# Pooling and three of four Q/K projections as seven products of quartered matrices, made ahead of attention

## The chip, the cores and the metric

One core of a Trainium2 chip runs the whole kernel. The metric is device time in microseconds (us) for one execution. The core's engines are TensorE (PE, matmul; its weight loads are listed as PEld), VectorE (DVE), ScalarE (ACT), GpSimd (POOL) and SyncE (SP, which issues most of the DMAs). Each takes its own instructions in the order of the program and waits at semaphores for the others.

## The reference, cut

```python
# x: 1 x 1024 x 1024, 8 heads of 64, 4 pooling groups of 128, D_FF = 2816, float32
h = rmsnorm(x, norm1_g)
proj = h @ w_in                       # [q | k | v | f_logit | u]
log_f = log_sigmoid(f_logit + b_forget); c = cumsum(log_f)
logits = q.k / 8 + c_t - c_s          # causal; p = softmax(logits)
attn = p @ v                          # per head
pooled_g = window_sum(u_g, w) / count - u_g     # w = 2, 4, 8, 16, one per group
pool = (pooled_g @ w_pool[g]) * pool_scale
x = x + concat(attn, pool) @ w_out
x = x + (silu(h2 @ w_gate) * (h2 @ w_up)) @ w_down        # h2 = rmsnorm(x, norm2_g)
y = rmsnorm(x, final_g)
```

## The kernel before

Every float32 operand of a matmul is split into a high part (an ACT copy into a rounded type) and a low part (source minus high, by DVE or POOL: `split`). A product is then three matmuls, `mm3`: high by high, high by low and low by high. A matmul has 128 rows of weights and moves up to 512 columns.

The stages, in order of time:

1. Rows of x are normalised, transposed and split into `hTh` and `hTl` (128 x 8 x 1024: eight chunks of the model's width, all 1024 frames). Beside this PE makes v for heads 0 to 3 and the forget logits `fl` (line L374).
2. Four pooling groups, `group_project`: for each, two halves of 512 frames by 8 chunks by 3 matmuls (48). Their sliding sums (`group_pool`) and splits run on DVE and POOL, the small matmuls by `w_pool` are `mix`, and `decay` makes the running sums of the forget gates, which go to DRAM as `augd`.
3. `project(0)` makes Q and K of the first pair of heads: two kinds, two halves, 8 chunks, 3 matmuls (96). The result is scaled and split; DMAs from SBUF to SBUF bring it into the stacks `s1` and `s2`, which hold high and low parts and `augd` rows one above the other, so that a score is two matmuls.
4. Attention: `attend(p, fill, counts)` runs eight jobs for each pair. A job is scores, minimum, exponential, normalisation, transposes and values. Between its steps it takes matmuls out of a generator, the fill, as many as `counts` says for each job. The fills are `project(1)`; `project(2)` and the rest of v; `project(3)`; and the first output rows, o4 and o6.
5. The remaining output rows, second norm and transposes.
6. Gate and up projections by seven products of quartered matrices, and the down projection, to the end.

The instructions of an engine run in the order in which the program has them. It follows the order of the code, moved by a scheduler where `issue_after` or a dependency asks for it. SP's queue is one of these orders: a DMA that waits for a buffer holds up all that stand behind it. `wmask` is a 128 x 1024 tile with the causal edge that every softmax reads (at L620).

Of the kernel before, what the change touches and what calls it, by code (L numbers as in the profile page):

```python
# [8 lines left out]
F32 = mybir.dt.float32  # L9
# [6 lines left out]
P = 128  # L16
# [29 lines left out]
def tile_kernel(  # L46
# [41 lines left out]
    def bank(name, tag, bufs, n=1):  # L88
# [26 lines left out]
    augd = dram.tile([H, 2 * AUG, S], F32, name="augd")  # L115

# [94 lines left out]

    with pool("early", "right") as ep:
        xts = {}

        def e2(name, dt=F32):
            return ep.tile([P, HALO + S], dt, tag="e2", bufs=9, name=name)

        def xload(tt):
            xts[tt] = ep.tile([P, D], F32, tag="x", bufs=4, name=f"x{tt}") if tt < 4 else e2(f"x{tt}")[:, 0:D]
            nc.sync.dma_start(out=xts[tt], in_=xf[tt * P : (tt + 1) * P, :])  # L220
# [7 lines left out]
        g8, gcol = e2("g8")[0:ND, 0:P], e2("gcol")[:, 0:ND]  # L228
# [16 lines left out]
        for tt in range(2, NT):  # L245
            xload(tt)
            if tt == 3:
                nc.sync.dma_start(out=bfb, in_=b_forget[0].partition_broadcast(P))
        junk = ep.tile([P, D], mybir.dt.bfloat16, name="junk")
# [22 lines left out]
        fl = ep.tile([P, NT, H], F32, name="fl")  # L272
# [108 lines left out]
        with tc.issue_after(mark["rstd"].ins):  # L381
            nc.gpsimd.dma_start(out=pscale, in_=pool_scale[0].rearrange("(g p) -> p g", p=P))


        def ft(name):
            return ep.tile([P, NT, H], F32, name=name)
# [20 lines left out]
        def decay():  # L407
            lfT = []
            for a in range(2):
                lfT.append(bank(f"lf{a}", "t", 4))  # L410
                for tt in range(4):
                    nc.tensor.transpose(lfT[a][0:H, tt * P : (tt + 1) * P], fs[:, 4 * a + tt, :], ident)
            def row(name, dt=F32):
                return ep.tile([P, S], dt, tag="x", bufs=4, name=name)[0:H, :]

            one, cc = row("one"), row("cc")
            zero = wmask[0:H, 0:512]
            chl = [row("chi", R), row("clo", R)]
            with tc.issue_after(mark["rstd"].ins):
                nc.gpsimd.memset(one, 1.0)  # L420
            for a in range(2):
                nc.vector.tensor_tensor_scan(
                    cc[:, a * 512 : (a + 1) * 512], lfT[a][0:H, :], zero,
                    0.0 if a == 0 else cc[:, 511:512], ALU.add, ALU.add,
                )
            split(chl[0], chl[1], cc)
            for n in range(2):
                chl.append(row(("nhi", "nlo")[n], R))
                nc.scalar.activation(out=chl[2 + n], in_=f32(chl[n]), func=AF.Copy, scale=-1.0)
            rows = [one, one, f32(chl[2]), f32(chl[3]), f32(chl[0]), f32(chl[1]), one, one]  # L430
            for n, row in enumerate(rows):
                (nc.sync if row is one else nc.gpsimd).dma_start(out=augd[:, n, :], in_=row)


        def mix(g):
            (ph, pl), (wph, wpl) = phl[g], wps[g]
            for tb in range(2):
                ts = slice(tb * 512, (tb + 1) * 512)
                ps = bank(f"m{g}_{tb}", *(("s", 4) if g > 1 else rotate("tp", 2)))
                mm3(ps, wph, wpl, ph[:, ts], pl[:, ts], True, True)  # L440
                if g > 1:
                    mo = e2(f"mo{g}_{tb}")[:, 0:512]
                else:
                    mo = ap_.tile([P, 512], F32, tag="th", bufs=4, name=f"mo{g}_{tb}")
                nc.scalar.activation(out=mo, in_=ps, func=AF.Copy, scale=pscale[:, g : g + 1])
                nc.sync.dma_start(out=mixd[NPAIR + g, :, ts], in_=mo)

        us, pfs, phl, wps = {}, {}, {}, {}

        def group_project(g, mid=None):  # L450
            with tc.issue_after(copies[NT - 1 if g < 3 else NT - 3].ins):
                wh, wl = wsplit(wpool, w_in_r[:, :, U0 + g * P : U0 + (g + 1) * P], f"u{g}", eng=nc.gpsimd)
            wh, wl = chunk(wh, P), chunk(wl, P)
            wpr = ep.tile([P, P], F32, tag="wpr", bufs=2, name=f"wpr{g}")
            nc.sync.dma_start(out=wpr, in_=w_pool[0, g])
            wpp, nb = (ep, 2) if g > 1 else (hpool, 2)
            wps[g] = [wpp.tile([P, P], R, tag=t, bufs=nb, name=f"{t}{g}") for t in ("wph", "wpl")]
            with tc.issue_after(copies[NT - 1].ins):
                split(*wps[g], wpr, nc.gpsimd)
            u = us[g] = e2(f"u{g}")  # L460
            nc.vector.memset(u[:, 0:HALO], 0.0)
            for tb in range(2):
                ts = slice(tb * 512, (tb + 1) * 512)
                ps = bank(f"u{g}_{tb}", "s", 4)
                for c in range(ND):
                    mm3(ps, wh[:, c, :], wl[:, c, :], hTh[:, c, ts], hTl[:, c, ts], c == 0, c == ND - 1)
                nc.scalar.activation(out=u[:, HALO + tb * 512 : HALO + (tb + 1) * 512], in_=ps, func=AF.Copy)
                if mid and tb == 0:
                    mid()

        def group_pool(g, eng):
            u, w = us[g], WINDOWS[g]
            prev, d = u, 1
            while d < w:
                nxt = e2(f"us{g}_{d}")
                if 2 * d < w:
                    nc.vector.memset(nxt[:, 0:HALO], 0.0)
                eng.tensor_tensor(
                    out=nxt[:, HALO:], in0=prev[:, HALO:], in1=prev[:, HALO - d : HALO + S - d], op=ALU.add
                )  # L480
                prev, d = nxt, 2 * d
            pf = pfs[g] = e2(f"pf{g}") if g > 1 else pf01[:, g, :]
            nc.vector.scalar_tensor_tensor(
                out=pf[:, HALO:S], in0=prev[:, 2 * HALO :], scalar=1.0 / w, in1=u[:, 2 * HALO :],
                op0=ALU.mult, op1=ALU.subtract,
            )
            nc.vector.tensor_tensor(
                out=pf[:, 0 : w - 1], in0=prev[:, HALO : HALO + w - 1], in1=rcount[:, 0 : w - 1], op=ALU.mult
            )
            nc.vector.tensor_scalar(  # L490
                out=pf[:, w - 1 : HALO], in0=prev[:, HALO + w - 1 : 2 * HALO], scalar1=1.0 / w, scalar2=None,
                op0=ALU.mult,
            )
# [936 lines left out]
```

## Time and profile before

| what | value |
|---|---|
| median of 3 runs | 1035.37 us (1034.99 to 1035.57) |
| span of the profiled execution | 1033.6 us |
| PE busy | 1024.3 us, 99% |
| DVE, ACT, POOL busy | 632.8, 454.2, 381.1 us |
| v done, groups begin | 38.8 us |
| attention with its fills, about | 118 to 350 us |
| gate and up | 410 to 818 us |

The span runs from the first to the last instruction of one profiled execution; the time of a run is taken around the whole execution. The profiled execution's own time is not listed apart from its span. A matmul's busy time in the rows overlaps with that of the next one, so what one costs is read from the distance between starts. In the rows, "out<-in" are the program's tiles, the number behind an engine's stretch is its busy time, and square brackets tell how long the engine had been idle and what ended it.

### The profile page before, as it was taken

To read this page: it belongs to the slowest core of one execution; us is meant where nothing else is said; L and a number is where in the kernel's file an instruction comes from. 1 tells how busy PE (TensorE), PEld (TensorE's weight loads), DVE (VectorE), ACT (ScalarE), POOL (GpSimd) and SP (SyncE) were. 2 spreads that over 40 slices of the span, in tenths; PEclk is the share of its full clock that TensorE was granted. 3 is DMA by queue.
4 is the path that set the end of the run, shared out by engine and by line. 5 is a ranking of instruction groups with operands and counts; after the bars stand their busy time and mean duration, and the time that the engine had idled before them with its cause. 6 is when DMAs were issued, how large, how long until landed. Compare 5 with 4: busy or idle time off the path is not lost.

```text
span 1033.6 us, 14202 instructions
## 1 busy us (share of the span) xinstructions
PE 1024.3 (99%) x5104; PEld 868.9 (84%) x5104; DVE 632.8 (61%) x1000; ACT 454.2 (44%) x733; POOL 381.1 (37%) x312
## 2 busy tenths in 40 slices
PE   9999999999999999999999999999999999999997
PEld 7988888998888888888888888888888888888886
DVE  7565566776886479744433334334334789788886
ACT  7434355665665257533333233233233343333346
POOL 4350121213346043447537536636637510000045
PEclk9999999999999999999999999999999999999999
DMA  7224434333643134343143143143236755353424
GB/s 251 53 47 143 105 81 103 84 102 89 224 175 106 49 136 129 103 143 112 62 132 113 62 133 112 64 131 113 81 113 251 248 204 175 110 198 97 153 92 163
DMA packets 108439, 130.21 MB, mean 126 GB/s; under 512 B 7369, under 2 KB 70353, under 8 KB 108369
## 3 DMA queue, kind: packets, MB, share of 16 engines
q1 hardware_dynamic: 96544, 108.18, 33.4%
q10 hardware_dynamic: 11504, 20.47, 5.2%
q8 instruction: 40, 0.66, 0.2%
q0 software_dynamic: 320, 0.66, 0.2%
q14 instruction: 31, 0.25, 0.1%
HBM read 86.29 MB, written 33.03 MB: 115 GB/s over the span
## 4 chain that ended last, share of the span: by engine, by line
PE 98%; DMA 1%; ACT 0%; DVE 0%; POOL 0%; issue 0%; ACTq 0%; POOLq 0%
PE gu_P L161 14%; PE gu_P L162 14%; PE gu_P L163 14%; PE d L161 7%; PE d L162 7%; PE d L163 7%; PE po L657 4%; PE tp L643 3%; PE o L161 3%; PE o L162 3%; PE qk L161 3%; PE qk L162 3%; PE qk L163 3%; PE o L163 3%; PE v L374 2%; PE z L618 2%
## 5 line engine op out<-in xcount | busy, mean ns | idle before, releaser
L121 DVE TENSOR_TENSOR gu_P_l<-s,gu_P_h 128x1024 fp32r<-128x1024 f32 (+1 forms) x48 | 66.5, 1393 | 98.6 <-ACT gu_P_h L120 98.5
L162 PE MATMUL d<-d,d 128*128 128x512 f32 (+1 forms) x308 | 119.5, 388 | 0.0
L163 PE MATMUL d<-d,d 128*128 128x512 f32 (+1 forms) x308 | 119.5, 388 | 0.0
L629 POOL TENSOR_SCALAR p<-p,rr 128x128 f32<-128x128 f32 (+3 forms) x64 | 48.6, 764 | 175.5 <-DVE rr L628 140.2
L161 PE MATMUL d<-d,d 128*128 128x512 f32 x308 | 107.8, 388 | 0.0
L120 ACT ACTIVATE d<-r_f 128x1536 fp32r<-128x1536 f32 (+1 forms) x28 | 38.8, 1384 | 117.6 <-PE d L162 101.6
L121 DVE TENSOR_TENSOR gu_P_l<-r,gu_P_h 128x1024 fp32r<-128x1024 f32 x32 | 48.9, 1527 | 64.3 <-ACT gu_P_h L120 64.3
L1063 POOL TENSOR_TENSOR s<-r 128x1024 f32<-128x1024 f32 x10 | 24.0, 2401 | 161.9 <-DMA r<-in_w_up_dram 116.0
L120 ACT ACTIVATE gu_P_h<-r 128x1024 fp32r<-128x1024 f32 x32 | 33.8, 1060 | 91.1 <-PE gu_P L162 35.5
L162 PEld LDWEIGHTS d<-d,d 128*128 128x128 f32 x308 | 57.8, 188 | 12.0 <-DVE d L121 0.2
L161 PEld LDWEIGHTS d<-d,d 128*128 128x128 f32 x308 | 57.8, 188 | 12.0
L163 PEld LDWEIGHTS d<-d,d 128*128 128x128 f32 x308 | 57.8, 188 | 11.9
L626 ACT ACTIVATE p<-p,mn 128x128 f32<-128x128 f32 (+3 forms) x64 | 49.3, 772 | 32.8 <-DVE mn L620 29.9
L1291 POOL TENSOR_SCALAR sse<-sse 128x1 f32<-128x1 f32 x7 | 3.5, 494 | 158.1 <-ACT junk L1287 158.1
L1150 POOL TENSOR_TENSOR h<-h,qh 128x512 f32<-128x512 f32 x33 | 44.3, 1345 | 32.3 <-ACT qh L1148 24.1
L648 DVE TENSOR_TENSOR tl<-tp,th 128x512 fp32r<-128x512 f32 (+1 forms) x80 | 49.3, 632 | 10.7 <-ACT th L647 9.7
L120 ACT ACTIVATE gu_P_h<-s 128x1024 fp32r<-128x1024 f32 (+1 forms) x48 | 47.0, 984 | 19.7 <-PE gu_P L162 13.0
L1147 DVE TENSOR_TENSOR qh<-gu_P,sn_sU 128x512 f32<-128x512 f32 x22 | 15.2, 690 | 60.5 <-POOL h L1150 43.2
L121 DVE TENSOR_TENSOR d<-r_f,d 128x1536 fp32r<-128x1536 f32 (+1 forms) x28 | 45.7, 1633 | 10.5 <-ACT d L120 10.5
L163 PE MATMUL qk<-hTh,l_qk 128*128 128x512 f32 x128 | 50.7, 396 | 0.0
L161 PE MATMUL qk<-hTh,h_qk 128*128 128x512 f32 x128 | 50.6, 395 | 0.0
L162 PE MATMUL qk<-hTl,h_qk 128*128 128x512 f32 x128 | 50.4, 394 | 0.0
(337 smaller groups left out, 3067.1 us busy)
## 6 DMA issues: line engine op xcount, KB each, us to landing
r_f<-hsdP SPq DMA_DIRECT2D x77, 256.0 KB
r_wd<-in_w_down_dram SPq DMA_DIRECT2D x22, 512.0 KB
hsdP<-f ACTq DMA_DIRECT2D x43, 256.0 KB
r<-in_w_gate_dram SPq DMA_DIRECT2D x21, 512.0 KB
r<-in_w_up_dram SPq DMA_DIRECT2D x21, 512.0 KB
s<-hi SPq DMA_DIRECT2D x64, 128.0 KB
hsdP<-h ACTq DMA_DIRECT2D x32, 256.0 KB
x<-in_x_dram SPq DMA_DIRECT2D x8, 512.0 KB
```

The source lines that it names most:

```text
L120: mark["hi"] = nc.scalar.activation(out=hi, in_=src, func=AF.Copy)
L121: return eng.tensor_tensor(out=lo, in0=src, in1=f32(hi), op=ALU.subtract)
L161: nc.tensor.matmul(ps, lh, rh, start=start, stop=False, **kw)
L162: nc.tensor.matmul(ps, lh, rl, start=False, stop=False, **kw)
L163: mark["mm"] = nc.tensor.matmul(ps, ll, rh, start=False, stop=stop, **kw)
L626: nc.scalar.activation(out=pr[:, :n], in_=pr[:, :n], func=AF.Exp, scale=-1.0, bias=mn, accum_out=rs)
L629: nc.gpsimd.tensor_scalar(out=pr[:, :n], in0=pr[:, :n], scalar1=rr, scalar2=1.0, op0=ALU.mult, op1=ALU.mult)
L643: nc.tensor.transpose(tp[:, w : w + P], probs[h, 2 * sb + a][:, s * P : (s + 1) * P], ident)
L648: nc.vector.tensor_tensor(out=tl[:, :w], in0=tp[:, :w], in1=f32(th[:, :w]), op=ALU.subtract)
L657: mark["pv"] = nc.tensor.matmul(po[:, first * P : 2 * P], vt[p][:, s, j, :], part[:, o : o + wd], start=(s == 0 and part is th), stop=(s = ...
L1063: g(out=s1, in0=a21, in1=a22, op=ALU.add)
L1150: nc.gpsimd.tensor_tensor(out=h, in0=h, in1=q, op=ALU.mult)
```

## The change

The four pooling groups, two at a time, and the Q and K columns of a pair of heads are taken as one 256-column weight block each. Its 2 x 2 quarters (two column halves, two halves of the model's width) and those of the transposed h (two halves of the width, two halves of the frames) are multiplied by seven products instead of eight. A product is 4 chunks by 3 matmuls. There are five such units: a (groups 3 and 2), b (groups 1 and 0), c (pair 0), e (pair 2) and f (pair 3). Together 420 matmuls replace 480. Pair 1 keeps `project(1)`.

- The right-hand sums and differences t1 to t4 of h's quarters are made once (`block_steps`): t1, t2 and t4 on DVE, t3 on POOL, their high parts on ACT, their low parts on DVE and (half of t3) POOL.
- The weight sums of a unit (`unit_sums`) are four 128 x 512 operations on POOL, for c on DVE. Each product's page is split by ACT and POOL (`unit_page`), three of them with the low part on DVE (`LOWS`).
- PSUM results are put together in SBUF by ACT copies and DVE additions (`unit_step`). For c, e and f `done` scales and splits each quarter and stores it to DRAM (`qkd`). The high part goes through `stage`, two halves of `wmask`; the mixed pooling outputs go through the same halves.
- `load_stacks` loads the stacks from `qkd`, eight DMAs for a head and a half of the frames; for pair 0 these are 32, issued ahead of attention.
- The causal edge of `wmask` is written at the stage's end instead of the kernel's start.
- The fills of attention move up: `project(1)`, then the rest of v, then o4 and o6 in steps of one `mm3`; their pages are prepared in halves of 512 on POOL.

```diff
+    GROUPS_OF = dict(a=(3, 2), b=(1, 0))
+    PAIR_OF = dict(c=0, e=2, f=3)
...
+    def unit_sums(u, eng):
...
+        eng.tensor_tensor(out=s1, in0=a21, in1=a22, op=ALU.add)
+        eng.tensor_tensor(out=a21, in0=a11, in1=a21, op=ALU.subtract)
+        eng.tensor_tensor(out=a11, in0=s1, in1=a11, op=ALU.subtract)
+        eng.tensor_tensor(out=a12, in0=a12, in1=a11, op=ALU.subtract)
...
+        n = page_count[0] % 3
+        page_count[0] += 1
+        if n == 2:
+            t = mid.tile([P, 2, 512], R, tag="page", bufs=1, name=f"w{u}_{k}")
+        else:
+            t = wpool.tile([P, 2, 512], R, tag="wl", bufs=2, name=f"w{u}_{k}")
+        pages1[u, k] = t
+        split(t[:, 0, :], t[:, 1, :], src, LOWS.get((u, k), nc.gpsimd))
...
+    MOVING = dict(P1=(0, 0), P2=(1, 0), P3=(1, 1), P6="t2", P5="t1", P7="t3", P4="t4")
...
+        for c in range(4):
+            ws = slice(c * P, (c + 1) * P)
+            mm3(ps, t[:, 0, ws], t[:, 1, ws], bh[:, c, :], bl[:, c, :], start and c == 0, stop and c == 3, True)
...
+    def stage(dt):
...
+        t = wmask[:, 512 * n : 512 * n + 512] if not late_stage or n == 0 else late_stage[0]
...
+        nc.scalar.activation(out=hi, in_=c, func=AF.Copy, scale=sc)
+        nc.vector.scalar_tensor_tensor(
+            out=low, in0=c, scalar=sc, in1=f32(hi), op0=ALU.mult, op1=ALU.subtract
+        )
+        for to, of_ in zip(qkd[f, PAIR_OF[u]], (hi, low)):
+            nc.sync.dma_start(out=to[:, ts], in_=f32(of_))
...
+        def difference(eng, tmp, b, a, q):
+            (bh, bl), (ah, al) = of(*b, q), of(*a, q)
+            return [go(eng, tmp, bh, ah), go(eng, tmp, tmp, bl, ALU.add), go(eng, tmp, tmp, al)]
...
+            mo = stage(F32)
+            nc.scalar.activation(out=mo, in_=ps, func=AF.Copy, scale=pscale[:, g : g + 1])
+            nc.sync.dma_start(out=mixd[NPAIR + g, :, ts], in_=mo)
...
+    FREE, BOUND = ("P1", "P2", "P3"), ("P6", "P5", "P7", "P4")
+    work = [("a", k) for k in FREE] + [("c", k) for k in FREE] + [(u, k) for k in BOUND for u in "ac"]
+    work += [(u, k) for u in "eb" for k in FREE + BOUND] + [("f", k) for k in BOUND + ("P1", "P3", "P2")]
...
-    attend(0, project(1), [5, 4, 4, 3, 8, 6, 6, 0])
-    attend(1, both(project(2), project_v23()), [10, 7, 6, 8, 10, 8, 12, 0])
...
-    attend(2, project(3, first_chunk), [5, 2, 1, 6, 14, 7, 7, 1])
...
-    attend(3, fill, [3, 3, 4, 4, 4, 4, 3, 2], drain=False)
...
+    attend(0, project(1), [5, 4, 4, 3, 6, 5, 5, 0])
...
+    attend(1, project_v23(), [5, 4, 5, 5, 4, 5, 4, 0], events=[
...
+    attend(2, fill, [3, 3, 4, 4, 5, 5, 5, 3], drain=False, events=[
...
+    attend(3, fill, [0, 3, 4, 5, 5, 5, 6, 5], drain=False, events=[
```

The places that matter below, as the program orders them. First DVE, from the last forget logit on. Before (the f... rows are the polynomial of the gates):

```order
L379 TENSOR_TENSOR fl<-v_7_567,bfb 128x8
L389 TENSOR_SCALAR fa<-fl 128x64
L403 TENSOR_SCALAR fm<-fl 128x64
L390 TENSOR_TENSOR fa<-fa,fl 128x64
L392 TENSOR_SCALAR fz_601<-fe 128x64
```

After, at the same place (sum_t4h and sum_t are sums of h's quarters, t1l and t2l low parts of such sums, wa_P a page of unit a):

```order
L411 TENSOR_TENSOR fl<-v_7_574,bfb 128x8
L557 TENSOR_TENSOR sum_t4h<-hTh 128x1024 x2
L604 TENSOR_SCALAR fa<-fl 128x64
L618 TENSOR_SCALAR fm<-fl 128x64
L557 TENSOR_TENSOR sum_t4h<-sum_t4h,hTl 128x1024 x2
```

and, some rows on:

```order
L557 TENSOR_TENSOR sum_t_618<-hTh,sum_t4h 128x1024
L608 RECIPROCAL fz_967<-fz_967 128x64
L572 TENSOR_TENSOR t1l_610<-sum_t4h,t1h_609 128x1024
L427 TENSOR_TENSOR r_c_148<-r_c_148 128x512
L557 TENSOR_TENSOR sum_t_617<-sum_t_617,hTl 128x1024
L126 TENSOR_TENSOR wa_P_730<-r_a_144,wa_P_730 128x512
```

The small rows of the gates now stand between 15 operations of 1024 columns, which end with t2l.

On POOL, from the first group's page on. Before (l_u is a page's low part, us the sliding sums):

```order
L121 TENSOR_TENSOR l_u_781<-r_u_778,h_u_780 128x1024
L478 TENSOR_TENSOR us_1_762<-u_642 128x1024
L478 TENSOR_TENSOR us_2_765<-us_1_762 128x1024
L478 TENSOR_TENSOR us_4_768<-us_2_765 128x1024
L478 TENSOR_TENSOR us_8_771<-us_4_768 128x1024
L121 TENSOR_TENSOR l_u_895<-r_u_892,h_u_894 128x1024
```

After (wc_P are pages of unit c, sum_t4l is t3's sum, t3l its low part):

```order
L126 TENSOR_TENSOR wc_P_659<-r_c_148,wc_P_659 128x512
L557 TENSOR_TENSOR sum_t4l<-sum_t4l,hTl 128x1024
L126 TENSOR_TENSOR wc_P_681<-r_c_148,wc_P_681 128x512
L557 TENSOR_TENSOR sum_t4l<-sum_t4l,hTl 128x1024 x3
L126 TENSOR_TENSOR wc_P_710<-r_c_148,wc_P_710 128x512
L572 TENSOR_TENSOR t3l_614<-sum_t4l,t3h_613 128x1024
L126 TENSOR_TENSOR wc_P_792<-r_c,wc_P_792 128x512
```

Four pages of 1024 have become a run of pages of 512 with t3's sums among them, and the sliding sums have left POOL.

On SP, at the way into attention. Before (s are the stacks, hi the scaled high part of Q or K in SBUF):

```order
L569 DMA s_0_1_0_1248<-hi_1_0_1363 64x512
L570 DMA s_0_1_0_1250<-hi_1_0_1363 64x512
L569 DMA s_0_1_1_1249<-hi_1_0_1363 64x512
L570 DMA s_0_1_1_1251<-hi_1_0_1363 64x512
L569 DMA s_0_1_0_1248<-hi_1_1_1557 64x512
```

After, the page load and the first of the 32 stack loads (qk_0h and qk_0l are pair 0's results in DRAM):

```order
L243 DMA r_f_1176<-in_w_in_dram 128x4x128
L173 DMA r_qk_1_1634<-in_w_in_dram 128x8x128
L782 DMA s_0_0_0_1470<-qk_0h 64x512
L783 DMA s_0_0_0_1470<-qk_0l 64x512
L784 DMA s_0_0_0_1471<-qk_0h 64x512
L785 DMA s_0_0_0_1471<-augd 4x512
```

and what stands behind the 32nd (qk_3h and qk_3l are f's results):

```order
L498 DMA qk_3h<-wmask 128x512
L498 DMA qk_3l<-r_f 128x512
L829 DMA s_0_1_0_1642<-augd 4x1024
L829 DMA s_0_1_1_1643<-augd 4x1024
L498 DMA qk_3h<-wmask 128x512
L498 DMA qk_3l<-r_f 128x512
L668 DMA mixd<-wmask 128x512 x2
```

The stores that empty `wmask` stand behind all loads of the stacks. The r_qk load reads into the buffer whose last reader is the page of f's P2.

PE at that place, after (fP is f's last product, z scores, qk_1 the fill):

```order
L168 MATMUL fP_1513<-hTh,wf_P_1510 128x512
L897 MATMUL z_0_0_1598<-s_1_0_0_1476,s_0_0_0_1470 128x128
L898 MATMUL z_0_0_1598<-s_1_0_0_1477,s_0_0_0_1471 128x128
L897 MATMUL z_1_0_1609<-s_1_0_0_1476,s_0_0_0_1470 128x256
L898 MATMUL z_1_0_1609<-s_1_0_0_1477,s_0_0_0_1471 128x256
L166 MATMUL qk_1_0_1646<-hTh,h_qk_1_1630 128x512
```

Four score matmuls are all that stands between the last product and the fill's first matmul.

584 lines of the change are left out of this document (398 added, 186 removed).

## The prediction

> **What bounds the kernel now.** I read the page's summary first, then the stretches of the span, then single instructions around the place of the change, and last the rows that price what the change adds.
>
> ```profile
> span 1033.6 us, 14202 instructions
> PE 1024.3 (99%) x5104; PEld 868.9 (84%) x5104; DVE 632.8 (61%) x1000; ACT 454.2 (44%) x733; POOL 381.1 (37%) x312
> PE 98%; DMA 1%; ACT 0%; DVE 0%; POOL 0%; issue 0%; ACTq 0%; POOLq 0%
> ```
>
> PE is 99% busy and the chain that ends last runs on it for 98%, so a matmul taken away is worth its time as long as nothing else starts to make PE wait. The stretches (each engine's busy us) show how much room the others have:
>
> ```profile
> core 0: us, PE busy (x) PEld busy (x) DVE busy (x) ACT busy (x) POOL busy (x), PEclk, DMA share, GB/s
> 0.00:41.00 41.00, 38.53 (x285) 35.30 (x286) 25.88 (x61) 27.11 (x62) 21.77 (x51) 1.00 0.61 191
> 41.00:66.00 25.00, 25.00 (x112) 20.66 (x111) 9.93 (x32) 4.73 (x8) 13.79 (x6) 1.00 0.08 22
> 66.00:90.00 24.00, 24.00 (x112) 19.78 (x110) 18.79 (x29) 12.14 (x16) 2.09 (x4) 1.00 0.33 87
> 90.00:128.00 38.00, 38.00 (x181) 32.01 (x180) 19.16 (x42) 15.04 (x28) 2.92 (x5) 1.00 0.49 130
> 128.00:348.00 220.00, 220.00 (x1380) 198.29 (x1379) 154.68 (x411) 128.16 (x273) 69.40 (x69) 1.00 0.39 114
> 410.00:818.00 408.00, 408.00 (x1802) 337.84 (x1801) 173.66 (x174) 145.57 (x194) 218.58 (x116) 1.00 0.36 120
> ```
>
> From 41 to 348 us PE never waits, and DVE and POOL are lightly used ahead of attention. The stage that already uses seven products, 410 to 818, fills PE too, with 174 + 219 = 392 us of DVE and POOL in 408.
>
> **What is saved.** Starts of matmuls price one of 512 columns:
>
> ```profile
> 38.84 0.40 PE L161 MATMUL u<-hTh,h_u 128*128 128x512 f32 x1
> ...
> 41.42 0.16 DVE L379 TENSOR_TENSOR fl<-v,bfb 128x8 f32<-128x8 f32 x1
> 41.61 0.39 PE L161 MATMUL u<-hTh,h_u 128*128 128x512 f32 x1
> ```
>
> Twelve steps lie between 38.84 and 41.61, so one costs 0.231 us. The four groups (4 x 48) and pairs 0, 2 and 3 (3 x 96) were 480 matmuls; five units of seven products of 12 are 420. 60 x 0.23 = 13.8 us saved. Everything from the last output rows on is unchanged and costs nothing.
>
> **What the product stage adds.** Ahead of attention now stand 420 + 24 = 444 matmuls and 8 small transposes: 444 x 0.23 + 0.6 = 102.7, from 38.84 to 141.5 us if nothing waits. DVE and POOL feed it. Their prices:
>
> ```profile
> 61.67 1.21 DVE L483 SCALAR_TENSOR_TENSOR pf<-us,u 128x1008 f32<-128x1008 f32 x1 [13.81 <-POOL us L478]
> 62.80 2.37 DVE L487 TENSOR_TENSOR pf<-us,rcount 128x15 f32<-128x15 f32 x1
> ...
> 65.20 1.20 DVE L478 TENSOR_TENSOR us<-u 128x1024 f32<-128x1024 f32 x1
> ...
> 66.35 0.15 DVE L494 TENSOR_TENSOR pf<-pf,u 128x16 f32<-128x16 f32 x1
> ```
> ```profile
> 61.81 3.32 POOL L121 TENSOR_TENSOR l_u<-r_u,h_u 128x1024 fp32r<-128x1024 f32 x1 [0.18 <-ACT h_u L120]
> ```
> ```profile
> 503.71 2.40 POOL L1063 TENSOR_TENSOR s<-r 128x1024 f32<-128x1024 f32 x1 [15.30 <-DMA r<-in_w_up_dram]
> 506.06 2.40 POOL L1065 TENSOR_TENSOR s<-r,r 128x1024 f32<-128x1024 f32 x1
> 508.42 1.29 POOL L1150 TENSOR_TENSOR h<-h,qh 128x512 f32<-128x512 f32 x1
> 509.67 2.42 POOL L1064 TENSOR_TENSOR s<-s,r 128x1024 f32<-128x1024 f32 x1
> ```
> ```profile
> 509.74 0.69 DVE L1147 TENSOR_TENSOR qh<-gu_P,sn_sU 128x512 f32<-128x512 f32 x1 [5.32 <-POOL h L1150]
> 510.35 0.68 DVE L1145 TENSOR_TENSOR h<-gu_P,qh 128x512 f32<-128x512 f32 x1
> ```
>
> By starts, DVE takes 1.15 us for 1024 columns and 0.61 for 512; POOL 2.36 and 1.25. The first rows show more: a POOL subtraction that began at 61.81, beside a DVE instruction with two SBUF inputs, took 3.32 instead of 2.40, and DVE's next one, of 15 columns, took 2.37 and ended when POOL did. The two run one after the other. The DVE row at 509.74, which has an input in PSUM, ran at its own 0.69 beside a POOL row of 2.42. So I charge DVE's two-SBUF instructions and POOL's to one common account.
>
> The new sums start when the last forget logit is written, at 41.6 (the L379 row). From there the order has, on the common account, DVE 42 x 1.15 + 17 x 0.61 = 58.7 us and POOL 7 x 2.36 + 41 x 1.25 + 4 x 0.46 = 69.6 us (the 128-column ones by a quarter of 1.25 and a start, an estimate). That is 128.3 us against PE's 102.7. The first place where it bites is P6 of units a and c: PE's 87th matmul of the stage needs the second half of t2's low part. PE would be there at 38.84 + 86 x 0.23 = 58.6. DVE's queue ahead of it holds 15 x 1.15 + 5 x 0.61 = 20.3; POOL can run 7 x 2.36 + 3 x 1.25 = 20.3 before its next page waits for a buffer that PE must free. Together 41.6 + 40.6 = 82.2: **a wait of 23.6 us**. With both engines at full speed it would be 41.6 + 20.3 + about 3 of DVE's other work = 65, a wait of 6.4.
>
> The Trainium skill's page "SBUF — State Buffer", section "Who interferes with whom", says that a VectorE instruction with two SBUF inputs and a GpSimd one that reads SBUF exclude one another through one shared port, for the whole instruction. By that rule the place comes at 82.2, without it at 65; the two long rows above agree with it.
>
> After that place PE has 358 matmuls and the transposes, 82.9 us, and the account 87.7, of which about 3 are DVE's behind POOL's last page. So that page (the low of f's P2) is done between 158.7 (PE never waits again: the page's buffer comes free 36 matmuls, 8.3 us, before the stage's end, and a copy and a subtraction take 1.9) and 166.9 (the account never idles). I take 163, the middle.
>
> **What the way into attention adds.** Before, stacks were filled beside matmuls. Now SP's queue holds, in order: a page load (r_qk, second kind) that waits for exactly that last low, then 32 stack loads, then the stores of f's results. These stores empty the two staging halves in wmask, and ACT's copies of the last mix wait for them; the first matmul of the fill (a "m" bank) waits for the copy of m0_1. So does the first softmax, through the mask that is rewritten behind the mix store. Prices:
>
> ```profile
> 92.78 0.26 SPq L549 DMA_DIRECT2D s<-augd  x1
> 93.14 0.53 SPq L569 DMA_DIRECT2D s<-hi  x1
> ...
> 94.35 0.59 SPq L569 DMA_DIRECT2D s<-hi  x1
> 94.98 0.59 SPq L570 DMA_DIRECT2D s<-hi  x1
> ```
> ```profile
> 350.16 0.33 SPq L865 DMA_DIRECT2D r_mix<-mixd  x1
> ...
> 353.12 0.63 ACT L120 ACTIVATE mix_h<-r_mix 128x512 fp32r<-128x512 f32 x1 [2.57 <-DMA r_mix<-mixd]
> ```
> ```profile
> augd<-chi POOLq DMA_DIRECT2D x1, 32.0 KB, 2.1
> ```
> ```profile
> L445 ACT ACTIVATE mo<-m,pscale x8: 682/690/690, 78.8 to 103.5; 128x512 f32<-128x512 f32 x8
> ```
>
> An issue into 64 rows takes 0.63 by starts, a load out of DRAM 0.33; a 64-row load is between, and I take 0.5 since both are near. 24 of them, 8 small ones at 0.3 and the page load at 0.4 make 14.8 us (10.7 to 18.2). A transfer lands 2.1 (POOL's queue) to 2.96 us (350.16 to 353.12) after its issue; I take 2.6. Then: store, landing 2.6, ACT copy 0.6, next store, landing 2.6, mix copy 0.69. From the last low to the fill's first matmul: 14.8 + 2.6 + 0.6 + 2.6 + 0.7 = 21.3 us (16.2 to 25.3), in which PE has 2 to 6 us of products and four score matmuls of 0.5 in all. PE resumes at 163 + 21.3 = 184.3 instead of 141.5 + 0.5 = 142.0: **42.3 us late**.
>
> **Inside attention** the 192 matmuls of two pairs (44 us) go. The stretch of 220 us becomes about 176, and DVE's share rises from 70% to at most 154.68 / 176 = 88%, ACT's to 73%. PE waits 0 to 5 us; 1.5 since it waits nowhere at 70%. The earlier loads of two units' weights stand behind the rows of x in SP's queue and are hidden by the first stage; if not, 1 us.
>
> **Sum:** -13.8 + 42.3 + 1.5 = +30.0 on the profiled span of 1033.6. The median of the runs, 1035.37, is 1.8 above that span, which I take as the time around it: 1065 us. Its own bounds: 158.7 + 16.2 gives +19 (1054), 166.9 + 25.3 + 5 gives +42 (1077).
>
> **Rivals.**
> A: DVE and POOL don't hold each other up here. Then the place at P6 costs 6.4, the last page is made at 141.5 + 6.4 - 6.4 = 141.5 and PE resumes at 162.8, 20.8 late: +8.5, 1044 us. Against it are the rows at 61.81 and 62.80; for it that the stage 410 to 818 carries both engines and fills PE, but there the account is 392 us of 408 at the very most and here it is 128 of 103.
> B: the account holds, but the way into attention is covered, because the copies find staging free. Then PE is only late by the stage, 167 - 141.5 = 25.5: +13.2, 1049 us. Against it: SP takes its queue in order.
> C, faster: the products keep pace because queues run ahead of PE, and the stack loads cost SP next to nothing. The place is SP's queue; the price is 16.2 at the low end, less the 6.9 that PE still has, 9.3; with A's 6.4 it is 15.7 against 13.8 saved. It decides once one load's issue falls under 0.25 us; at 0.1 it is 1032, with everything covered 1035.37 - 13.8 = 1021.6. Against it: the 64-row issues above take 0.53 and 0.59.
> D: the thinner fill makes DVE the bound of attention: above 90% of 176 us PE waits with it, 10 us on top of the sum, 1075.
>
> **How the numbers follow.** The sum 0.55, A 0.16, B 0.10, C 0.13, D 0.06. The likeliest gives 1065. The range, 1036 to 1080, reaches into A and leaves out most of C and the far end of D. About 0.2% (2 us) is what a measurement of this kernel can tell from no change: faster 0.13, within it 0.04 (the upper end of C), slower 0.83.
>
> **What would show it.** Right: PE idle about 24 us near 58 us, released by DVE's t2l; long POOL and DVE rows side by side there; PE idle again 12 to 20 us before the first qk matmul of the fill, behind a row of some 32 SP issues; PE without gaps after. Wrong: POOL rows of 1.25 and 2.4 beside two-SBUF rows of DVE; stack loads issued well before the last page; PE gaps inside attention. The forecast fails most if the stage's engines overlap or if SP issues a 64-row load in under 0.3 us.

## The result, and the profile after

The changed kernel takes 1105.32 us (median of 4 runs, 1102.71 to 1108.06) against 1035.47 (1034.99 to 1036.52) before on the same chip: the ratio is 1.067, 95% interval 1.065 to 1.0691. It is slower, as forecast, but by 69.9 us and not by 30. The span of the profiled execution is 67.3 us longer.

The summary and the chain of work that ended last, of the kernel after:

```profile
span 1100.9 us, 14323 instructions
PE 1037.5 (94%) x5044; PEld 867.7 (79%) x5044; DVE 705.2 (64%) x1037; ACT 480.2 (44%) x789; POOL 471.4 (43%) x374
PE 80%; DVE 10%; SPq 3%; ACT 2%; issue 2%; DMA 2%; POOL 1%; POOLq 0%; ACTq 0%; DVEq 0%
```

PE executes 60 matmuls fewer and is yet busy for 13 us more. Its share of the chain fell from 98 to 80%; DVE carries 10% now and SP's queue 3%. Where, is seen in the stretches (busy us of each engine, then the granted clock of TensorE as a share of full speed, DMA share and GB/s):

```profile
core 0: us, PE busy (x) PEld busy (x) DVE busy (x) ACT busy (x) POOL busy (x), PEclk, DMA share, GB/s
0.00:44.80 44.80, 38.45 (x275) 35.78 (x276) 31.88 (x59) 25.90 (x58) 23.63 (x50) 0.96 0.50 169
44.80:60.00 15.20, 12.97 (x55) 10.05 (x54) 14.32 (x10) 2.31 (x5) 13.68 (x7) 0.97 0.00 1
60.00:85.00 25.00, 8.37 (x24) 5.64 (x23) 25.00 (x22) 10.65 (x15) 11.71 (x5) 0.68 0.15 41
85.00:100.00 15.00, 15.00 (x59) 12.21 (x60) 14.96 (x20) 6.26 (x10) 5.93 (x4) 0.89 0.11 37
100.00:195.00 95.00, 80.79 (x320) 62.01 (x319) 63.70 (x78) 37.40 (x60) 61.99 (x43) 0.93 0.39 118
195.00:208.00 13.00, 0.91 (x5) 0.62 (x3) 1.92 (x2) 2.54 (x4) 0.00 (x0) 0.63 0.73 249
208.00:412.00 204.00, 200.96 (x1279) 178.96 (x1280) 147.58 (x421) 128.62 (x289) 83.36 (x91) 0.99 0.43 126
476.00:884.00 408.00, 408.00 (x1802) 337.95 (x1801) 173.90 (x172) 144.25 (x193) 218.89 (x116) 1.00 0.35 119
```

From 60 to 85 us PE does 24 matmuls beside a DVE that is full; from 195 to 208 it does almost nothing while DMAs move 249 GB/s. The clock is under 1.00 in the stretches around these waits. Gate and up hold the same 1802 matmuls in 408 us (476 to 884) as before (410 to 818).

Busy time hides half of it, so I made a sum of another kind from the matmul rows: a stage's length less 0.2284 us for every 512 columns that its matmuls move is the time that PE lost there. (Some loss is the fixed cost of short matmuls; the stage before from 38.84 to 112.56 us gives -0.1, which shows how exact the sum is.) In e7_all and e8_pesums the first product begins before the last of v, so their first two rows share the work otherwise. Each cell is length / lost, in us:

| stage, up to | before | after | e1_dve | e7_all | e8_pesums |
|---|---|---|---|---|---|
| first product | 38.8 / 10.3 | 44.8 / 16.4 | 44.9 / 16.3 | 37.3 / 11.4 | 38.3 / 11.3 |
| first score | 73.7 / -0.1 | 150.2 / 48.2 | 121.3 / 19.4 | 124.8 / 20.3 | 122.8 / 10.4 |
| fill's first matmul | in the stage above | 13.0 / 12.7 | 13.4 / 13.0 | 2.2 / 1.9 | 1.4 / 1.1 |
| last values product | 237.3 / 22.5 | 204.1 / 33.0 | 208.6 / 37.3 | 207.9 / 36.5 | 206.4 / 35.0 |
| gate and up | 46.4 / 2.5 | 50.8 / 5.4 | 51.5 / 6.0 | 52.6 / 7.3 | 48.8 / 3.5 |
| all lost | 35.2 | 115.7 | 92.0 | 77.4 | 61.3 |

After loses 80.5 us more than before and has 13.8 us less to do: 66.7, the distance by which gate and up begin later (462.96 against 396.22). All of the difference but 0.6 us is in this table. Counted matmul by matmul, the losses of the first row and of the attention come out 0.2 to 0.5 us higher in every column, so a few tenths mean nothing there.

**The first rows.** DVE's normalisation of the last row of x, POOL's rows beside it, and PE's wait:

```profile
28.68 6.73 DVE L395 SCALAR_TENSOR_TENSOR x<-x,rstd_a,g1b 128x1024 f32<-128x1024 f32 x1
...
29.35 1.31 POOL L424 TENSOR_TENSOR u<-r_a 128x512 f32<-128x512 f32 x1
...
30.62 2.47 POOL L126 TENSOR_TENSOR wa_P<-r_a,wa_P 128x512 fp32r<-128x512 f32 x2
...
33.06 1.25 POOL L425 TENSOR_TENSOR r_a<-r_a,r_a 128x512 f32<-128x512 f32 x1
34.40 2.15 POOL L426 TENSOR_TENSOR r_a<-u,r_a 128x512 f32<-128x512 f32 x1
...
35.55 0.66 PE L155 MATMUL tr_a<-ident,x 128*128 128x128 f32 x2 [4.61 <-DVE x L395]
```

A DVE instruction that costs 1.28 alone (e2_early below) took 6.73: unit a's sums and pages, now on POOL at this place, go through one behind the other, and DVE gets its turn only after the fourth (34.31); the fifth takes 2.15 instead of 1.25, beside DVE. PE waits 4.61 for it, and the first product begins at 44.83 instead of 38.84.

**P6 and the clock.** The PE rows that waited, with the ones behind them:

```profile
58.92 0.78 PE L168 MATMUL cP<-hTh,wc_P 128*128 128x512 f32 x1 [1.98 <-POOL wc_P L126]
59.50 0.63 PE L166 MATMUL cP<-hTh,wc_P 128*128 128x512 f32 x1
59.93 0.63 PE L167 MATMUL cP<-hTl,wc_P 128*128 128x512 f32 x1
...
62.45 0.39 PE L167 MATMUL cP<-hTl,wc_P 128*128 128x512 f32 x1
62.68 0.40 PE L168 MATMUL cP<-hTh,wc_P 128*128 128x512 f32 x1
75.82 0.79 PE L166 MATMUL cP<-hTh,wc_P 128*128 128x512 f32 x1 [12.75 <-ACT wc_P L125]
...
84.89 0.50 PE L167 MATMUL aP<-t2l,wa_P 128*128 128x512 f32 x1 [3.54 <-DVE t2l L572]
```
```profile
74.43 0.67 DVE L427 TENSOR_TENSOR r_c<-r_c 128x512 f32<-128x512 f32 x1
```
```profile
75.14 0.63 ACT L125 ACTIVATE wc_P<-r_c 128x512 fp32r<-128x512 f32 x1 [2.72 <-DVE r_c L427]
```
```profile
78.46 3.36 DVE L557 TENSOR_TENSOR sum_t<-sum_t,hTl 128x1024 f32<-128x1024 f32 x1
...
85.50 1.21 DVE L572 TENSOR_TENSOR t2l<-sum_t,t2h 128x1024 fp32r<-128x1024 f32 x1
```

PE stands still three times, 18.3 us in all. The longest wait, 12.75, is for the page of c's P3, the product ahead of a's P6: ACT's copy waits for the weight sum r_c, which stands in DVE's queue among the sums of h. The last one, 3.54, is for t2l. DVE's sum at 78.46 takes 3.36 instead of 1.21, beside POOL. And the starts behind a wait are 0.43 us apart instead of 0.23, for some 3 us, at once or (behind 84.89) some 1.6 us later. From 45 to 213 us some 45 matmuls start at that distance and lose some 9 us together, beside the waits.

**The way into attention.** The last page on POOL, ACT's copy for it, SP's queue, the copies that wait for a store, and PE:

```profile
180.51 0.63 ACT L125 ACTIVATE wf_P<-r_f 128x512 fp32r<-128x512 f32 x1 [3.38 <-PE fP L168]
```
```profile
181.22 1.28 POOL L126 TENSOR_TENSOR wf_P<-r_f,wf_P 128x512 fp32r<-128x512 f32 x1 [2.71 <-ACT wf_P L125]
```
```profile
182.53 0.38 SPq L173 DMA_DIRECT2D r_qk<-in_w_in_dram  x1
183.01 0.55 SPq L782 DMA_DIRECT2D s<-qk_0h  x1
...
201.21 0.48 SPq L785 DMA_DIRECT2D s<-augd  x1
201.79 0.35 SPq L498 DMA_DIRECT2D qk_3h<-wmask  x1
```
```profile
204.17 0.63 ACT L493 ACTIVATE wmask<-r_f 128x512 fp32r<-128x512 f32 x1 [8.21 <-DMA qk_3h<-wmask]
...
207.37 0.69 ACT L667 ACTIVATE wmask<-m,pscale 128x512 f32<-128x512 f32 x1 [1.23 <-DMA qk_3h<-wmask]
```
```profile
208.11 0.80 PE L166 MATMUL qk<-hTh,h_qk 128*128 128x512 f32 x1 [12.20 <-ACT wmask L667]
```

The order of the prediction, step for step: last low done at 182.50, page load, 32 stack loads, store, ACT copy, store, mix copy, first matmul of the fill.

### The profile page after: what moved, and what is told of

The parts are those of the page before. It is cut to its first block, busy times and chain, and to the rows that moved or that the text cites. A ratio compares the mean times of both kernels' runs of the same rounds, so it can differ in the third digit from the quotient of the medians.

```text
span 1100.9 us, 14323 instructions
## 1 busy us (share of the span) xinstructions
PE 1037.5 (94%) x5044; PEld 867.7 (79%) x5044; DVE 705.2 (64%) x1037; ACT 480.2 (44%) x789; POOL 471.4 (43%) x374
## 4 chain that ended last, share of the span: by engine, by line
PE 80%; DVE 10%; SPq 3%; ACT 2%; issue 2%; DMA 2%; POOL 1%; POOLq 0%; ACTq 0%; DVEq 0%
PE gu_P L167 13%; PE gu_P L166 13%; PE gu_P L168 13%; PE d L166 6%; PE d L168 6%; PE d L167 6%; PE po L937 3%; PE tp L923 3%; PE o L166 2%; PE o L167 2%; PE o L168 2%; DVE sum_t4h L557 1%; DVE us L679 1%; PE z L897 1%; PE z L898 1%
## 5 line engine op out<-in xcount | busy, mean ns | idle before, releaser
L125 ACT ACTIVATE d<-r_f 128x1536 fp32r<-128x1536 f32 (+1 forms) x28 | 38.8, 1384 | 117.8 <-PE d L167 107.4
L928 DVE TENSOR_TENSOR tl<-tp,th 128x512 fp32r<-128x512 f32 (+1 forms) x80 | 49.8, 633 | 14.8 <-ACT th L927 14.2
L1448 DVE TENSOR_TENSOR qh<-gu_P,sn_sU 128x512 f32<-128x512 f32 x22 | 15.2, 689 | 59.6 <-POOL h L1451 42.8
L927 ACT ACTIVATE th<-tp 128x512 fp32r<-128x512 f32 (+1 forms) x80 | 42.6, 551 | 23.6 <-PE tp L923 21.7
L1686 DVE TENSOR_TENSOR x2f_s<-d,x2f_s 128x512 f32<-128x512 f32 x64 | 42.6, 684 | 11.4 <-PE d L168 11.4
L923 PE MATMUL tp<-ident,p 128*128 128x128 f32 x288 | 45.0, 275 | 1.1 <-DVE tl L928 0.8
```

The source lines that it names most:

```text
L125: mark["hi"] = nc.scalar.activation(out=hi, in_=src, func=AF.Copy)
L923: nc.tensor.transpose(tp[:, w : w + P], probs[h, 2 * sb + a][:, s * P : (s + 1) * P], ident)
L927: nc.scalar.activation(out=th[:, :w], in_=tp[:, :w], func=AF.Copy)
L928: nc.vector.tensor_tensor(out=tl[:, :w], in0=tp[:, :w], in1=f32(th[:, :w]), op=ALU.subtract)
L1686: added = nc.vector.tensor_tensor(out=row, in0=ps, in1=row, op=ALU.add)
```

## The experiments

Twelve kernels, each in three rounds against the kernel before. The theory: PE loses its time to POOL holding up DVE (start, P6, the pages up to the stage's end), to SP's queue on the way into attention, and to the clock behind each wait. Rivals stand in each expectation.

**e1_dve** and **e2_early** take POOL's part of the stage apart.

```diff
-    LOWS.get((u, k), nc.gpsimd)
+    LOWS.get((u, k), nc.gpsimd if u == "a" and k in ("P1", "P2", "P3") else nc.vector)
-    unit_sums(u, nc.vector if u == "c" else nc.gpsimd)
+    unit_sums(u, nc.gpsimd if u == "a" else nc.vector)
-    unit_sums("f", nc.gpsimd)
+    unit_sums("f", nc.vector)
-    V, G = nc.vector, nc.gpsimd
+    V, G = nc.vector, nc.vector
```

> All of the product stage's POOL work except unit a's sums and its first three pages goes to DVE: the other pages' low parts, the weight sums of e, b and f, and t3's sums. Port theory (DVE's two-SBUF instructions and POOL's exclude one another, so the stage is paced by their sum): DVE does a 512-column operation in 0.61 us where POOL takes 1.25, so the sum falls from 128 to about 92 us, and DVE's queue with its PSUM additions (about 30 x 0.61) and small rows becomes the bound at about 116. t2's second low part ends near 46.2 + 20.3 + 6.9 + 1.8 = 75 instead of 86.7 us, and the last score-free product ends 15 to 25 us earlier: 1080 to 1090 us in all. Rival (each engine's own queue order paces the stage, not a shared port): DVE gets 33 us more, t2's low part ends about 9 us later than 86.7, and the kernel is 5 to 30 us slower than 1105.

1079.31 us, ratio 1.0422 (1.0401 to 1.0442): 26 us less than after and just under the range expected, by giving nearly all of it to one engine. PE's waits and the stage's last low:

```profile
66.60 0.80 PE L166 MATMUL cP<-hTh,wc_P 128*128 128x512 f32 x1 [7.57 <-ACT wc_P L125]
74.78 0.80 PE L166 MATMUL aP<-t2h,wa_P 128*128 128x512 f32 x1 [6.96 <-ACT t2h L571]
```
```profile
160.68 0.69 DVE L126 TENSOR_TENSOR wf_P<-r_f,wf_P 128x512 fp32r<-128x512 f32 x1
```

t2l is ready at 78.52 instead of 86.71 (the sums begin at the same 46.3), and from there to the last low it is 82.85 us instead of 95.8. PE loses 19.4 us in the stage instead of 48.2. POOL beside DVE cost more than it carried: a page's low takes DVE 0.69 us and POOL 1.28, and the two-input work of DVE waits meanwhile.

```diff
-    order.enter_context(tc.issue_after(copies[NT - 3].ins))      # a's first three pages
+    order.enter_context(tc.issue_after(copies[NT - 1].ins))
-    order.enter_context(tc.issue_after(mark["rstd"].ins))        # unit_sums
+    order.enter_context(tc.issue_after(copies[NT - 1].ins))
```

> Unit a's first pages and its sums on POOL wait for the last high copy of the transposed rows instead of starting beside the rows' normalisation. Port theory: the normalisation of row 7 on DVE (two SBUF inputs, 6.73 us in the changed kernel) was held by five POOL instructions one behind the other; it now takes 1.2, v ends near 39 instead of 44.8, the sums start near 41.6 and all that follows moves up: 4 to 6 us less, 1099 to 1101 us. Rival (the row waited for its data or its factor): the row keeps its 6.7 us and nothing moves, 1105.

1104.78 us, 1.0667 (1.0644 to 1.069): nothing, where the theory expected 4 to 6 us. The cause of the long row is as said:

```profile
30.33 1.28 DVE L395 SCALAR_TENSOR_TENSOR x<-x,rstd_a,g1b 128x1024 f32<-128x1024 f32 x1
```
```profile
180.89 1.28 POOL L126 TENSOR_TENSOR wf_P<-r_f,wf_P 128x512 fp32r<-128x512 f32 x1 [2.71 <-ACT wf_P L125]
```

The normalisation takes 1.28, the sums start at 41.95 (46.25 after), t2l ends at 82.27 (86.71), the last product of unit b starts 4.2 us earlier. But the last low begins at 180.89 instead of 181.22. What was won is waited away in the last unit, whose pages wait in turn for PE, ACT and POOL. An early gain is worth its length only if every later bound moves with it.

**e3_loads16** and **e5_split** are on the way into attention.

```diff
-        for half in range(2):
-            for j in range(2):
-                load_stacks(0, j, half)
+        for j in range(2):
+            load_stacks(0, j)            # 16 loads of 1024 columns instead of 32 of 512
```

> The stacks of pair 0 are loaded in 16 DMAs of 1024 columns instead of 32 of 512; the same bytes. Queue theory (PE's wait ahead of the fill is SP's issue time: 32 issues in 18.8 us from 183.0 to 201.8, then the stores that free the staging halves): 16 issues take about 9.5, PE's wait of 12.2 us falls to about 3 and the half-pace after it shortens: 8 to 10 us less, 1095 to 1097 us. Rival (the wait is for the bytes or for landings): the wait stays near 12 us, 1103 to 1106.

1100.69 us, 1.0636 (1.0608 to 1.0664): 4.6 us less, between the range of the theory and that of the rival; the interval overlaps that of after a little. Half the issues, but not half the time:

```profile
195.63 0.44 SPq L783 DMA_DIRECT2D s<-qk_0l  x1
196.12 0.48 SPq L784 DMA_DIRECT2D s<-augd  x1
197.05 0.35 SPq L498 DMA_DIRECT2D qk_3h<-wmask  x1
```
```profile
203.50 0.63 ACT L493 ACTIVATE wmask<-r_f 128x512 fp32r<-128x512 f32 x1 [5.56 <-DMA qk_3h<-wmask]
```
```profile
207.15 0.79 PE L166 MATMUL qk<-hTh,h_qk 128*128 128x512 f32 x1 [9.37 <-ACT wmask L667]
```

The loads take 12.5 us of the queue instead of 18.8, but the copy that waits for the store behind them starts 6.4 us after the store's issue instead of 2.4, and PE still waits 9.37 us. The DMA share is 1.00 from 197.0 to 203.5 us here, and 0.59 from 195 to 202 in after. So in after the bound is the issues, and the bytes stand close behind it.

```diff
-        for half in range(2):
-            for j in range(2):
-                load_stacks(0, j, half)
+        load_stacks(0, 0, 0)             # the 8 that the first scores read
...
-    attend(0, project(1), [5, 4, 4, 3, 6, 5, 5, 0])
+    attend(0, project(1), [5, 4, 4, 3, 6, 5, 5, 0], events=[
+        (0, lambda: load_stacks(0, 0, 1)), (1, loads(0, 1)),
+    ])
```

> Of the 32 loads of pair 0's stacks only the 8 that the first scores read stay behind the last raw page; the other 24 (16 of them wide, or 8 of 512 and 8 of 1024 columns) go behind the product loop in the code. Theory (the fill's first matmul waits for a bank whose reader waits for a store that stands behind the loads on SP's queue): the copy L667 comes about 14 us earlier, the 12.2 us idle time at 208 shrinks to under 2 us and the half pace after it (2.6 us) goes too: 1091 to 1096 us. Rival (the stores' landing, or the bytes, set the fill's start whatever stands ahead of them): the wait stays at 8 us or more, 1100 to 1106 us.

1095.64 us, 1.0574 (1.0556 to 1.0591): 9.7 us less, at the theory's end. The store now stands behind 8 loads:

```profile
189.99 0.41 SPq L783 DMA_DIRECT2D s<-augd  x1
192.40 0.95 SPq L498 DMA_DIRECT2D qk_3h<-wmask  x2
```
```profile
199.88 0.79 PE L166 MATMUL qk<-hTh,h_qk 128*128 128x512 f32 x1 [2.38 <-ACT wmask L667]
```

The wait is 2.38 instead of 12.20, though the same bytes move. The half pace stayed, against the theory: a wait of 2.38 us, some 7 us behind one of 3.77, was enough for it.

**e4_warm** and **e6_warm** are on the clock. e4 puts 40 needless matmuls behind the first scores:

```diff
+            idle = bank("idle", "po", 1)
+            for _ in range(40):
+                nc.tensor.matmul(idle, hTh[:, 0, 0:P], hTh[:, 0, 0:512], start=True, stop=True)
```

> 40 matmuls of 512 columns into an unused bank stand behind the first four score matmuls, in PE's wait ahead of the fill; their result isn't used. Clock theory (after a wait of 2 us or more PE runs at half pace, 0.43 instead of 0.23 us a matmul, for 3 to 4 us): the fill's first 11 matmuls run at 0.23, 2 to 2.5 us less after the wait. Rival (the slow matmuls wait for their operands): they stay at 0.43 and nothing is gained.

1108.1 us, 1.0697 (1.068 to 1.0714).

```profile
213.36 0.48 PE L923 MATMUL tp<-ident,p 128*128 128x128 f32 x1 [8.17 <-POOL p L909]
```

It does not decide on the clock: the scheduler placed the first transposes ahead of the fill, PE waited 8.17 us for POOL's normalised probabilities behind the 40 matmuls, and the fill began at 214.16, at 0.43 us a matmul. e6 is the cleaner one, on top of e1:

```diff
+    zeros = mid.tile([P, P], R, name="zeros")
+    nc.gpsimd.memset(f32(zeros), 0.0)
+    IDLE = {("c", "P3"): ("c", "c1", 38), ("a", "P6"): ("a", "c1", 28)}
...
+        for m in range(count):           # ahead of that product; adds zero to an open sum
+            nc.tensor.matmul(chains[v, at], zeros, hTh[:, m % 4, 0:512], start=False, stop=False, skip_group_check=True)
```

> e1_dve with 66 matmuls by a tile of zeros (28 added into a's open sum, 38 into c's, 0.23 us each, 15.2 us in all) in the two waits of TensorE before P6, so that it is never idle there for 2 us. Theory (after an idle time of about 2 us TensorE runs at half its pace for some 3.5 us, whatever it multiplies): the first matmuls of c's P3 and of a's P6 follow at 0.23 us instead of 0.43; the granted clock between 60 and 85 us rises from about 0.7 to over 0.9; the time is 1075 to 1079 us, since VectorE is 97 to 100% busy up to 106 us and sets the pace of most of what follows. Rival (the half pace comes from the operands, just written by VectorE, or from its access to memory): the pitch stays at 0.43, the time is 1079 to 1083 us.

1077.93 us, 1.0406 (1.0387 to 1.0424). The same stretch, of e1_dve first and then of e6_warm:

```profile
60.00:85.00 25.00, 11.44 (x37) 8.51 (x37) 25.00 (x32) 10.78 (x14) 0.00 (x0) 0.66 0.22 64
```
```profile
60.00:85.00 25.00, 25.00 (x109) 20.17 (x108) 25.00 (x32) 12.32 (x18) 0.00 (x0) 1.00 0.22 63
```

The granted clock goes from 0.66 to 1.00, and the starts behind P6 are 0.23 apart. So idle time makes the half pace, not the operands. The Trainium skill's page "TensorE: Matmul & The Clock Gate" (Part 1, the HAM clock gate) says that the array's clock is halved after an idle window of about 3.4 us and full again after as long a busy one. The halved clock and the 3 to 5 us of its length agree with these rows; the waits that set it off were as short as 1.98 us, while two of 2.49 and 2.58 us in e5_split set none off. The time hardly changed (the two ranges overlap), most likely since DVE, full in this stretch of both, sets when the work after it can go on.

**e7_all** joins e1, e2 and e5.

> e1_dve (product stage's POOL work on VectorE) with unit a's pages and sums behind the last row's copies (as e2_early) and the loads split (as e5_split). Theory (with POOL out of the way nothing between P6 and the stage's end swallows an earlier start, and the transition is a queue): 4.3 us from the start and 8 to 11 us from the transition off 1079.3 us: 1064 to 1068 us. Rival (VectorE, 97 to 100% busy to 106 us, sets the stage, so that the earlier start is lost, and the transition's wait is bytes): 1074 to 1080 us. Neither reaches 1035 us: what is left is TensorE's wait for VectorE before P6 (some 14 us), VectorE's account of the stage, and the attention with fewer products beside it (some 12 us).

1064.11 us, 1.0258 (1.0233 to 1.0283), 15.2 us under e1. Here the early start, worth nothing in e2, counts: the first score is made 4.1 us earlier than in e1, and the rest, 11.1 us, comes from the way into attention.

**e8_pesums** makes t1 and t2 on PE, inside its own wait:

```diff
+            for n, (sign, x) in enumerate(parts):      # t2 = h11 - h01 + h00, t1 = h01 - h00, high and low parts
+                nc.tensor.matmul(ps, sign, x, start=n == 0, stop=n == len(parts) - 1)
+            nc.scalar.activation(out=hi, in_=ps, func=AF.Copy)
+            V.tensor_tensor(out=lo, in0=ps, in1=f32(hi), op=ALU.subtract)
```

> e7_all with t1 and t2 summed by TensorE in PSUM (40 matmuls by plus or minus the identity, 9.2 us at 0.23) instead of by VectorE (10 operations of 128x1024, some 1.2 us each, gone from before P6; t4 then takes one operation more for each half, and the lows are read from PSUM). Theory (TensorE's wait before P6, 14.9 us and 3.4 us of half pace in e7_all, is VectorE's account up to P6): P6 starts 10 to 13 us earlier, the added matmuls lie in the wait: 1050 to 1056 us. Rival (the wait comes from the pages, copied by ScalarE and split on VectorE, and not from the sums): the wait stays above 9 us and the added matmuls come on top: 1062 to 1072 us.

1057.44 us, 1.0211 (1.0194 to 1.0228). The same stretch of e7_all, then of e8_pesums:

```profile
60.00:75.00 15.00, 6.02 (x13) 4.30 (x14) 15.00 (x20) 4.20 (x6) 0.00 (x0) 0.50 0.29 90
```
```profile
60.00:75.00 15.00, 13.75 (x58) 10.62 (x59) 14.75 (x26) 8.23 (x13) 0.00 (x0) 1.00 0.36 105
```

Up to 75 us PE waits 1.3 us in place of 14.9: the wait was DVE's sums. Unit a ends 7.4 us earlier; at the first score only 0.9 of that is left (most likely again the last units' pages), and the time fell by 6.7, less than expected, the rest of it found in the attention (1.5 us shorter) and the last output rows (3.8; these take 48.6 to 52.7 us in kernels that have the same code there, so this part may not be e8's own).

**e9_fill, e10_prep, e11_best, e12_look** ask what the attention loses.

```diff
 e9, on e7:   attend(3, fill, [0, 3, 4, 5, 5, 5, 6, 5], ...)  ->  [2, 5, 6, 7, 7, 7, 6, 5]
 e10, on e8:  prepare(..., eng=nc.gpsimd)  ->  eng=nc.vector, and the first pages' "mix" lows too
 e11:         e10 with the quotas of e9
 e12, on e8:  LOOK = 1  ->  2, attend(0, ...) quotas [6, 5, 5, 4, 6, 6, 0, 0]
```

> e7_all with the last attention group's quotas of fill raised from 0, 3, 4, 5, 5, 5, 6, 5 to 2, 5, 6, 7, 7, 7, 6, 5, so that 12 steps of 3 matmuls of 512 columns (8.2 us of TensorE's work) move from behind the last values product into the attention. Theory (with fewer products beside it, the attention leaves TensorE without work in gaps too short to be shown as waits, 36.5 us of its 208 in e7_all against 20.8 of 208 before, so that fill there costs less than its length): the stretch behind the last values product gets 8 us shorter and the attention 3 to 6 us longer: 1058 to 1062 us. Rival (the matmuls themselves run slower there, so that fill costs its length): 1063 to 1066 us.

1061.39 us, 1.0249 (1.0233 to 1.0264), 2.7 under e7, but the two ranges overlap (1060.28 to 1063.23 and 1059.74 to 1064.5). It lies in the theory's range, but not by its mechanism: the attention got 7.1 us longer for 8.2 us of added matmuls, and lost 35.6 us, as much as without them (36.5). The gain is in the output rows behind it, 41.9 us instead of 52.6.

> e8_pesums with the lows of the output projection's pages in the attention (22 operations on POOL, some 33 us of it) on VectorE. Theory (the attention's extra loss of TensorE's time, 35.0 us against 22.5 before, is again POOL's work that holds up VectorE's rows of the softmax and the probabilities' lows): the loss falls to 24 to 29 us, the time to 1047 to 1052 us. Rival (the loss comes from the chain of scores, softmax and transposes with fewer products beside it, and VectorE has the more to do): the loss stays within 3 us of 35, 1055 to 1061 us.

1056.93 us, 1.0206 (1.0191 to 1.0221): the rival. The loss is 34.1 us. So POOL's lows are not what costs PE its time here, unless what they take from VectorE and what VectorE has more to do now cancel.

> e10_prep with the last group's raised quotas of fill (as e9_fill): 2 to 4 us under e10_prep if the two edits do not share a cause (e9_fill took 2.7 us off e7_all), so 1044 to 1049 us by the theory of POOL in the attention, 1052 to 1058 us by its rival. Neither reaches 1035 us.

1057.53 us, 1.021 (1.0192 to 1.0227): the rival's range; on this kernel the quotas brought nothing.

> e8_pesums with each job's scores made two jobs ahead instead of one (and the first group's fill moved one job forward for it, 6, 5, 5, 4, 6, 6, 0, 0). Theory (the attention loses TensorE's time because with fewer products the next job's probabilities are not ready in time: a chain of scores, softmax, scaling and transposes): the loss in the attention falls from 35.0 us to 24 to 30, the time to 1047 to 1053 us. Rival (every short matmul costs more than its columns, or VectorE's 85 to 90% sets the pace): the loss stays within 3 us of 35, 1055 to 1061 us.

1056.56 us, 1.0201 (1.0184 to 1.0218): the rival again; deeper look-ahead doesn't help. So the attention's part stays open. The rows say this much. Counted matmul by matmul, one distance exceeds its columns by over 0.1 us before, and 52 do after, by 11.2 us together, about the 10.5 of the table. The first 11 of them, 2.2 us, are the half pace behind the wait of 12.20. For six, 3.3 us, the trace names a releaser, and it is DVE each time (tl, at, x_r, l_wo). For the other 35 it names none.

No version reached the kernel before; the best four lie at 1056.6 to 1057.5. In e8 PE still loses 26.1 us more than before and does 9.1 us of sums, against 13.8 saved.

## Why the prediction was wrong by 37 us

Against the span the forecast was +30.0, the result is +67.3. By its own steps:

- **Saved, 13.8 us: right.** The losses of the table and this saving add up to the result, and gate and up are unchanged.
- **The account up to P6: right, 40.46 us** from the sums' start (46.25) to the end of t2l (86.71), predicted 40.6. Rival A, DVE and POOL side by side at full speed, falls with it, and with e1. That it fits to 0.1 us is in part luck: some 2.5 us of DVE's other rows (two additions out of PSUM and the small rows of the gates) are in the 40.46 and were not in its terms.
- **The start: wrong, 4.6 us.** The sums were to start at 41.6 and started at 46.25. The prediction costed only the loads of the moved weights (0 to 1 us), and did not follow POOL's moved sums and pages into the first rows, where they hold up DVE by the same rule that it charged for at P6; with them behind the rows' copies (e2) the sums start at 41.95. A step that is moved must be priced at its new place.
- **From P6 to the last low: wrong by 15.0 us.** Predicted 80.8 (82.2 to 163), measured 95.8 (86.71 to 182.50), beyond the upper bound. It took the middle of two limits, 76.5 (PE never waits again) and 84.7 (the account never idles), as if one of the two always ran. This is the step that failed most: neither did. From 86.71 to 182.50 a POOL row or a DVE row with two inputs in SBUF is in progress for 83.4 us, so the account stands still for 12.4. From 95 to 195 us PE waits 14.2 us: 4.5 for pages, 4.5 for DVE's additions to finished products, 3.9 for a copy into `wmask`, 1.3 for a mix. It loses 9 more in matmuls that start late without a wait that the trace names; 22 of them, at the half pace, make 4.3 of it. No step of the sum had any of this. That the few buffers make the engines wait for one another by turns is read from the rows (at 180.51 a page's copy waits 3.38 us for PE); no kernel with more buffers was run, so this part of the cause is argued. With POOL out of the way (e1) the same stretch takes 82.85, inside the two limits.
- **The way into attention: the mechanism right, 4.3 us too short**, 25.6 (182.50 to 208.11) against 21.3. The mis-sized term is the loads: 14.8 us by an issue of 0.5, measured 19.3 (182.53 to 201.79). A 64-row load takes 0.61 of the queue in the mean (0.49 to 0.93 by starts), near the 0.63 of the loads out of SBUF, and the 8 small ones 0.52 instead of 0.3. The rest of the chain came to 6.3 us, predicted 6.5.
- **Attention and output rows: wrong by 13.5 us**, 15.0 against 1.5. The table shows 10.5 lost in the attention and 2.9 in the rows; 0.6 comes behind the start of gate and up, and 1.0 is rounding in the forecast's own base (142.0 with 0.23 us a matmul; 0.2284 gives 141.05). The step that failed is the 1.5 us for PE's waits there: it had only DVE's share to go by. Rival D had the kind right, priced it at 10 and gave it 0.06 as a case of its own; it came on top. DVE's share of the stretch from 208 to 412, bounded at 88%, is only 72%, and that does not keep short waits away. Why the attention loses more is not shown (e9 to e12).

4.6 + 15.0 + 4.3 + 13.5 = 37.4, the 37.3 that were missing. These four errors have one sign: each stage was charged for the wait that ends last in it, and not for what the other engines add when buffers tie them together. The forecast's upper bound of 1077 (the range ends at 1080) came from the extremes of three terms: the last low, the way, and 5 us in the attention. The start had 1 us at most, and the slow matmuls behind a wait had no term.

The outlook of the prediction held in part. The long DVE rows beside POOL and the idle time behind 32 issues are there. The idle time near P6 is there with 18.3 us instead of 24, but t2l ends only the last 3.54 of it; 12.75 stand one product earlier, at c's P3, whose weight sum waits in the same DVE queue and which the prediction did not look at. "PE without gaps after" did not hold.

## What to carry to other kernels

Saved matmuls are worth their time only where nothing else gets work: here 60 matmuls (13.8 us) came with 72 us more busy time of VectorE and 90 of GpSimd (held rows included), much of it rows that exclude one another, at a place where TensorE had never waited. Before giving work to GpSimd, ask what VectorE does in the same microseconds; here nearly all of the stage's GpSimd work on VectorE instead was 26 us faster (e1_dve). Keep the stores that free a buffer ahead of bulk loads in a queue, and price each longer wait of TensorE with the slow matmuls that may stand behind it.

## What the runs showed of the hardware

- **Half pace after short waits.** Behind seven waits of 1.98 to 12.75 us in the changed kernel, matmuls of 512 columns start 0.43 us apart instead of 0.23, for 3 to 5 us, some 1.3 us lost for each. Not every short wait does it: two of 1.13 and 1.24 us there, and two of 2.49 and 2.58 in e5_split, were followed by the full pace. Filled with matmuls by zero, the stretch before P6 keeps the clock at 1.00 (e6_warm).
- **A DVE row can be held by several POOL rows in a row.** One of 1.28 us was held for 6.73 while four POOL instructions went through (28.68 in after). From 46 to 69 us the two took turns, and DVE rows of 1.2 us took 2.3 to 3.5. A DVE row of 64 columns with one input, in SBUF, was held there too (2.40 at 50.73); one with an input in PSUM was not (0.68 at 62.18).
- **A store lands late behind wide loads.** The copy that waits for it starts 6.4 us after its issue behind 16 loads of 1024 columns, 2.4 behind 32 of 512 (e3_loads16 and after).
